# First layer's attention: probabilities scaled while they are turned, by products with a scaled unit matrix

## The chip, the cores and the metric

The kernel runs as one program on one core of a Trainium2 chip. The metric is the device time of one execution in microseconds; shown is the median of several executions. The numbers of the profile come from one execution that the hardware profiler recorded.

## What is computed

The reference is a trunk of two layers over 512 latent tokens and 256 context tokens of width 1024. The first layer runs global attention (eight heads of 64, in two groups that share keys and values) beside a bidirectional RWKV-7 recurrence; the second runs windowed attention beside a state-space mixer. Each layer ends in an MLP. The change is in the first layer's attention, which for a block of queries is:

```python
def block(q):
    s_lat = jnp.einsum('bqgrd,bkgd->bgrqk', q, kl).astype(F32) * scale
    s_ctx = jnp.einsum('bqgrd,bkgd->bgrqk', q, kc).astype(F32) * scale
    p_lat, p_ctx = joint_softmax([s_lat, s_ctx])
    return (jnp.einsum('bgrqk,bkgd->bqgrd', p_lat.astype(vl.dtype), vl)
            + jnp.einsum('bgrqk,bkgd->bqgrd', p_ctx.astype(vc.dtype), vc))
```

The context tokens attend to the context alone, in the same form.

## The kernel before

Everything is F32 on 128 partitions. Tokens are cut into six tiles of 128: tiles 0 and 1 are context, 2 to 5 latent. The order of instructions on each engine is not written out: the code is traced into a list, and a scheduler of the tile framework, which plays a timeline forward, places each instruction on its engine. Code under `tc.high_priority()` (the steps of the recurrence) goes first. Each engine then works through its own list in order.

The stage around the change is the second `with` block (line 886 on). Two things are woven into each other there by generators: the recurrence (`state_mixing`, 12 blocks with two steps each; its products are `z`, `xv`, `x`, `u`, `s` and `y`, lines 985 to 1072) and attention (`attend`, line 1127, one call per tile in the order 0, 1, 3, 4, 2, 5). At its end `finish` normalises the recurrence's output, tile by tile, and turns it (`yt`, line 1116).

`attend` works per tile on two groups of four heads. For each head the scores go into `sc` (line 1147), VectorE finds the row's maximum into `st` (line 1149), ScalarE takes the exponential into `prob` with the row sum beside it (line 1154), VectorE inverts the sum (line 1155), and ScalarE multiplies the whole row of `prob`, 768 columns for a latent tile and 256 for a context tile, by the inverse (line 1156). Then `weighted` (line 323) goes through the tiles of keys, two for a context tile and six for a latent one: four transposes of 128x128, one per head, into one tile `pt` of PSUM (line 332), a copy to SBUF into `pts` by VectorE or ScalarE (lines 335 and 337), and a product with the values into `po` (line 341). These products come in pairs: the first of a pair uses the first 64 columns of the array and writes the upper half of `po`, the second the other columns and the lower half. Lines 344 and 345 add the halves. The second layer's `attend1` calls `weighted` too.

Raw weights are loaded from HBM by SP into three buffers of 128x1024 with the tag `wraw` (line 283) and split into a high and a low part (`split`: ScalarE line 279 into `whi`, VectorE line 280 into `wlo`, two buffers each). After the stage comes the output product `wout` (line 1302), for the context tokens first, then two groups of latent tiles: for each group the mixers' output is loaded back from DRAM (`raw`, line 1293), split into `xr` and other places, and multiplied by eight tiles of weights that go through `wraw`. The queries `qr` and `qs` of `attend` sit in the buffers with the tags `whi` and `wlo`.

Of the kernel before, what the change touches and what calls it, by code (L numbers as in the profile page):

```python
# [10 lines left out]
F32 = mybir.dt.float32  # L11
F32R = mybir.dt.float32r
AF = mybir.ActivationFunctionType
# [5 lines left out]
P = 128  # L19
# [205 lines left out]
def tile_trunk(ctx: ExitStack, tc: tile.TileContext, t: dict, out, cc: Cols, pc: Cols):  # L225
    nc = tc.nc
    V, A, G, T = nc.vector, nc.scalar, nc.gpsimd, nc.tensor

    def pool(name, bufs=1, space=bass.MemoryType.SB, stack=ctx, side="left"):
        waits = "pool" if space == DRAM else "tile"  # L230
        return stack.enter_context(tc.tile_pool(name=name, bufs=bufs, space=space, side=side, reuse_waits=waits))
# [3 lines left out]
    def u(s):  # L235
        uid[0] += 1
        return f"{s}_{uid[0]}"

    cp = pool("const")
    wp = pool("weights")  # L240
# [8 lines left out]
    def K(name, a=0, n=None):  # L249
        s, w = cc.at[name]  # L250
        return cst[:, s + a:s + (w if n is None else a + n)]

    def Q(name, a=0, n=None):
        s, w = pc.at[name]
        return par[:, s + a:s + (w if n is None else a + n)]

    ident, ones = K("ident"), K("ones")
# [8 lines left out]
    def psum(tag, name):  # L266
        if isinstance(banks[tag], str):
            tag = banks[tag]
        v = banks[tag]
        if isinstance(v, list):  # L270

            v.append(v.pop(0))
            v = v[0]
        p, bufs, n, tag = v
        return p.tile([P, 512 * n], F32, tag=tag, name=u(name), bufs=bufs)
# [15 lines left out]
    def cols2(seg):  # L291

        return slice(256 + seg[0], 256 + seg[0] + seg[1])
# [29 lines left out]
    def weighted(prob, vt, g, kts, o, pool):  # L323

        r, po, n = HALVES[g], psum("po", "po"), len(kts)
        pair = []
        for m, kt in enumerate(kts):
            pt = psum("pt", "pt")  # L330
            for j in range(4):
                T.transpose(pt[:, P * j:P * j + P], prob[j][:, P * m:P * m + P], ident)  # L332
            w = pool.tile([P, 512], F32, tag="pts", name=u("pts"), bufs=3)
            if m % 2 == 1:
                V.tensor_copy(out=w, in_=pt)
            else:
                A.activation(out=w, in_=pt, func=AF.Copy)
            pair.append((m, kt, w))
            if len(pair) == 2 or m == n - 1:
                for i, (m_, k_, w_) in enumerate(pair):  # L340
                    T.matmul(po[HALVES[i], :], lhsT=vt[:, k_, r], rhs=w_, start=m_ < 2, stop=m_ + 2 >= n, tile_position=(0, 64 * i))  # L341
                pair = []
            yield
        A.activation(out=o[r], in_=po[HALVES[1], :], func=AF.Copy)
        V.tensor_tensor(out=o[r], in0=po[HALVES[0], :], in1=o[r], op=ALU.add)
# [540 lines left out]
    with ExitStack() as sb:  # L886
# [240 lines left out]
        def attend(qi, keys):  # L1127

            kt0, kt1 = keys
            c0, c1 = 256 + P * kt0, 256 + P * kt1  # L1130

            qr = wp.tile([P, 1024], F32R, tag="whi", name=u("qr"), bufs=2).bitcast(F32).rearrange("p (h c) -> p h c", h=8)
            for o in HALVES:
                nc.sync.dma_start(qr[o], qD[0:4, :, P * qi:P * qi + P].rearrange("j (g q) c -> q (j g) c", g=2))
            qs = wp.tile([P, 1024], F32R, tag="wlo", name=u("qs"), bufs=2).rearrange("p (h c) -> p h c", h=8)
            A.activation(out=qs, in_=qr, func=AF.Copy)
            V.tensor_tensor(out=qs[64:128], in0=qr[64:128], in1=qs[64:128].bitcast(F32), op=ALU.subtract)
            o = tp.tile([P, 512], F32, tag="oa", name=u("oa"), bufs=1)
            for g in (0, 1):
                prob = []  # L1140
                for j in range(4):
                    ps = psum("sc", "sc")
                    for s in SEGS:
                        if s[0] >= P * kt1:
                            continue
                        for m, kx in enumerate((kh, kl)):
                            T.matmul(ps[:, cols2(s)], lhsT=qs[:, 2 * j + g, :], rhs=kx[:, g, s[0]:s[0] + s[1]], start=m == 0, stop=m == 1)  # L1147
                    st = tp.tile([P, 4], F32, tag="st", name=u("st"), bufs=6)
                    V.tensor_reduce(out=st[:, 0:1], in_=ps[:, c0:c1], op=ALU.max, axis=AX.X)
                    sc = sq8[:, qi, 2 * j + g:2 * j + g + 1]  # L1150
                    V.tensor_scalar(out=st[:, 1:2], in0=st[:, 0:1], scalar1=sc, scalar2=-1.0, op0=ALU.mult, op1=ALU.mult)
                    pr = tp.tile([P, NT], F32, tag="prob", name=u("prob"), bufs=5)
                    pv = pr[:, 0:c1 - c0]
                    A.activation(out=pv, in_=ps[:, c0:c1], func=AF.Exp, scale=sc, bias=st[:, 1:2], accum_out=st[:, 2:3])
                    V.reciprocal(out=st[:, 3:4], in_=st[:, 2:3])
                    A.activation(out=pv, in_=pv, func=AF.Copy, scale=st[:, 3:4])
                    prob.append(pr)
                    yield
                yield from weighted(prob, vtok, g, list(range(kt0, kt1)), o, tp)
            nc.scalar.dma_start(oD[0:4, :, P * qi:P * qi + P].rearrange("a q c -> q a c"), o.rearrange("p (a c) -> p a c", c=P))  # L1160
# [105 lines left out]
    with ExitStack() as sc:  # L1266
# [8 lines left out]
        scale = norm_scale(0, 4, "nmlp")  # L1275
# [67 lines left out]
    st = ctx.enter_context(ExitStack())  # L1343
# [6 lines left out]
    def M(name):  # L1350
        return msk[:, mc.at[name][0]:sum(mc.at[name])]

    psum_pool(sd, "right", sc=(1, 2), pt=(1, 1), po=(1, 1))
    with ExitStack() as sh:
# [64 lines left out]
        pk, pv, pb = project((CTX_SEG, *LATS), 8, 9, 0)  # L1419
# [27 lines left out]
        for k in range(KT):  # L1447
            for q, (a, b) in enumerate(((dwh, hh), (dwh, hl), (dwl, hh))):
                for s in SEGS:
                    T.matmul(ps[0:16, cols2(s)], lhsT=a[:, 16 * k:16 * k + 16], rhs=b[:, k, s[0]:s[0] + s[1]],  # L1450
                             start=k == 0 and q == 0, stop=k == KT - 1 and q == 2)
        dr_ = temp("dtraw")
        V.tensor_copy(out=dr_[0:16], in_=ps[0:16, 256:1024])
        pt = psum("s", "dtT")
# [29 lines left out]
        pt = psum("s", "acs")  # L1484
# [17 lines left out]
        def attend1(qi):  # L1502

            lo, hi = max(2, qi - 1), min(NTT, qi + 2)
            n = hi - lo
            kts = [0, 1] + list(range(lo, hi))
            o = tp.tile([P, 640], F32, tag="prob", name=u("oa"), bufs=6)[:, 0:512]
            for g in (0, 1):
                prob = []
                for j in range(4):  # L1510
                    hd = 4 * g + j
                    q = q1[:, g, j, P * (qi - 2):P * (qi - 2) + P]
                    ps = psum("sc", "sc")
                    for m, kx in enumerate((k1h, k1l)):
                        T.matmul(ps[:, 256:512], lhsT=q, rhs=kx[:, g, 0:NCTX], start=m == 0, stop=m == 1)
                        T.matmul(ps[:, 512:512 + P * n], lhsT=q, rhs=kx[:, g, P * lo:P * hi], start=m == 0, stop=m == 1)
                    pr = tp.tile([P, 640], F32, tag="prob", name=u("prob"), bufs=6)
                    pv = pr[:, 0:256 + P * n]
                    A.activation(out=pv, in_=ps[:, 256:512 + P * n], func=AF.Copy, scale=0.125)
                    for kt, m in ((qi - 1, "neg0"), (qi + 1, "neg1")):  # L1520
                        if lo <= kt < hi:
                            blk = pr[:, 256 + P * (kt - lo):256 + P * (kt - lo) + P]
                            G.tensor_tensor(out=blk, in0=blk, in1=M(m), op=ALU.add)
                    st = tp.tile([P, 6], F32, tag="st", name=u("st"), bufs=5)
                    V.tensor_reduce(out=st[:, 0:1], in_=pv, op=ALU.max, axis=AX.X)
                    V.tensor_scalar(out=st[:, 1:2], in0=st[:, 0:1], scalar1=-1.0, scalar2=nsink[:, hd:hd + 1], op0=ALU.mult, op1=ALU.min)
                    A.activation(out=pv, in_=pv, func=AF.Exp, bias=st[:, 1:2], accum_out=st[:, 2:3])
                    A.activation(out=st[:, 3:4], in_=Q("sink", hd, 1), func=AF.Exp, bias=st[:, 1:2])
                    V.tensor_tensor(out=st[:, 4:5], in0=st[:, 2:3], in1=st[:, 3:4], op=ALU.add)
                    V.reciprocal(out=st[:, 5:6], in_=st[:, 4:5])  # L1530
                    A.activation(out=pv, in_=pv, func=AF.Copy, scale=st[:, 5:6])
                    prob.append(pr)
                    yield
                yield from weighted(prob, vt1, g, kts, o, tp)

            split(*(q1[:, m, :, P * (qi - 2):P * (qi - 2) + P] for m in (0, 1)), o.rearrange("p (a c) -> p a c", c=P))
# [209 lines left out]
    with ExitStack() as se:  # L1746
# [6 lines left out]
        scale = norm_scale(1, 4, "nmlp")  # L1753
# [50 lines left out]
```

## Time and profile before

| | before |
|---|---|
| median of 3 runs | 2008.97 us (2008.75 to 2009.16) |
| profiled execution | 2009.51 us |
| its span, first to last instruction | 2007.7 us |
| mean granted clock of TensorE | 0.975 |
| bytes read from HBM / written | 200.00 MB / 25.96 MB |
| queue of the loads by SP and ScalarE (q1), share of 16 engines | 36.1% |

The profile gives for each engine the time in which it had work in hand, and groups of like instructions with their count, mean duration and the idle time ahead of them. A name such as `pt<-cst,prob` says which tile is written and which are read; `cst` is the tile of constants that holds the unit matrix. PE is TensorE and PEld its weight loads, DVE VectorE, ACT ScalarE, POOL GpSimd, SP SyncE, which issues loads and stores. The granted clock is the share of TensorE's full speed that the chip allowed. Records of matmuls overlap, since the next starts before the one ahead has drained, so beside a record's duration the time from one start to the next is of use.

### The profile page before, as it was taken

How to read it: one execution, taken by the hardware profiler on the slowest of the kernel's cores; microseconds unless marked ns; L12 is line 12 of the kernel's file. 1: busy time of each engine (PE TensorE's matmuls, PEld its weight loads, DVE VectorE, ACT ScalarE, POOL GpSimd, SP SyncE). 2: the span in 40 equal slices, each digit the busy share in tenths (PEclk: the TensorE clock that was granted, in tenths of full speed). 3: DMA queues.
4: the chain of work that ended last, by engine and by line, in shares of the span. 5: the costliest groups of instructions: out<-in, count | busy, mean ns of one | idle time of the engine just before them, and what ended most of it. 6: DMA issues, size and time to landing. Idle time of an engine off the chain costs nothing.

```text
span 2007.7 us, 34218 instructions
## 1 busy us (share of the span) xinstructions
PE 1896.6 (94%) x13992; PEld 1545.1 (77%) x13992; DVE 1215.2 (61%) x2150; ACT 840.7 (42%) x1419; POOL 294.2 (15%) x291
## 2 busy tenths in 40 slices
PE   6999988899998999999999999899899789999997
PEld 4776756776765998888888889778578488888886
DVE  5567979775677765654544444865687464444445
ACT  3344442555544552232223224544566454333335
POOL 0000014432321520000000002310153120000001
PEclk9999998899998999999999999999999799999998
DMA  9355575742414733344444422212101133333333
GB/s 336 121 166 171 182 228 148 156 89 56 98 44 132 251 107 99 122 124 136 125 125 121 136 84 80 76 53 74 32 1 53 32 95 105 95 92 97 95 97 113
DMA packets 147884, 228.18 MB, mean 114 GB/s; under 512 B 65024, under 2 KB 102288, under 8 KB 147600
## 3 DMA queue, kind: packets, MB, share of 16 engines
q1 hardware_dynamic: 140912, 213.54, 36.1%
q10 hardware_dynamic: 5456, 7.73, 1.1%
q0 software_dynamic: 1360, 4.73, 0.7%
q8 instruction: 110, 1.80, 0.4%
q14 instruction: 46, 0.38, 0.1%
HBM read 200.00 MB, written 25.96 MB: 113 GB/s over the span
## 4 chain that ended last, share of the span: by engine, by line
PE 77%; DVE 9%; DMA 7%; ACT 3%; issue 3%; POOL 1%; SPq 0%; DVEq 0%; POOLq 0%; ACTq 0%
PE m L367 37%; PE win L367 13%; PE po L341 4%; DMA wmod<-in_wmod_dram 4%; PE pt L332 3%; PE z L985 2%; DVE wlo L280 2%; PE sc L1147 2%; PE wout L1718 1%; PE wout L1302 1%; PE s L1051 1%; PE mod L405 1%; PE lora L653 1%; PE z L1560 1%; DVE junk L1319 1%
## 5 line engine op out<-in xcount | busy, mean ns | idle before, releaser
L279 ACT ACTIVATE whi<-wraw 128x1024 fp32r<-128x1024 f32 x214 | 226.4, 1059 | 678.0 <-PE m L367 561.0
L280 DVE TENSOR_TENSOR wlo<-wraw,whi 128x1024 fp32r<-128x1024 f32 x214 | 264.4, 1236 | 212.2 <-ACT whi L279 209.4
L367 PE MATMUL m<-hh,whi 128*128 128x512 f32 (+1 forms) x816 | 239.3, 344 | 4.9 <-ACT relu L1241 2.4
L367 PE MATMUL m<-hl,whi 128*128 128x512 f32 (+1 forms) x816 | 241.2, 343 | 0.2 <-POOL hl L503 0.2
L367 PE MATMUL m<-hh,wlo 128*128 128x512 f32 (+1 forms) x816 | 241.3, 344 | 0.0
L367 PE MATMUL m<-dl,whi 128*128 128x256 f32 (+1 forms) x832 | 240.7, 341 | 0.0
L367 PE MATMUL m<-dh,whi 128*128 128x256 f32 (+1 forms) x832 | 238.6, 342 | 1.7 <-DVE xl L1223 1.6
L367 PE MATMUL m<-dh,wlo 128*128 128x256 f32 (+1 forms) x832 | 239.8, 341 | 0.1
L367 PEld LDWEIGHTS m<-dh,whi 128*128 128x128 f32 x832 | 153.3, 188 | 23.9 <-DVE xl L1223 4.9
L367 PEld LDWEIGHTS m<-hh,whi 128*128 128x128 f32 x816 | 152.1, 188 | 24.7 <-ACT relu L1241 2.8
L471 POOL TENSOR_TENSOR acc<-acc,nsq 128x256 f32<-128x256 f32 x42 | 42.8, 1027 | 865.8 <-ACT nsq L470 861.0
L367 PEld LDWEIGHTS m<-hl,whi 128*128 128x128 f32 x816 | 153.6, 188 | 19.4 <-POOL hl L503 0.4
L367 PEld LDWEIGHTS m<-dl,whi 128*128 128x128 f32 x832 | 153.8, 188 | 19.0
L367 PEld LDWEIGHTS m<-dh,wlo 128*128 128x128 f32 x832 | 153.7, 188 | 18.9 <-DVE wlo L280 0.3
L367 PEld LDWEIGHTS m<-hh,wlo 128*128 128x128 f32 x816 | 153.4, 188 | 19.0 <-DVE wlo L280 0.3
L367 PE MATMUL win<-hl,whi 128*128 128x512 f32 (+1 forms) x512 | 162.3, 348 | 4.7 <-POOL hl L503 3.5
L367 PE MATMUL win<-hh,whi 128*128 128x512 f32 (+1 forms) x512 | 162.3, 362 | 2.7 <-ACT hh L498 2.7
L367 PE MATMUL win<-hh,wlo 128*128 128x512 f32 (+1 forms) x512 | 160.2, 345 | 0.0
L1319 DVE SCALAR_TENSOR_TENSOR junk<-wmod,crow 128x1024 f32<-128x1024 f32 x64 | 78.5, 1226 | 118.5 <-DMA wmod<-in_wmod_dram 117.9
L1223 DVE SCALAR_TENSOR_TENSOR xl<-m,modT,xl 128x512 f32<-128x512 f32 (+1 forms) x144 | 97.4, 686 | 72.3 <-PE m L367 72.3
L367 PEld LDWEIGHTS win<-hh,whi 128*128 128x128 f32 x512 | 95.4, 194 | 33.6 <-issue 15.7
L367 PEld LDWEIGHTS win<-hl,whi 128*128 128x128 f32 x512 | 98.5, 193 | 22.9 <-issue 5.7
(413 smaller groups left out, 3560.0 us busy)
## 6 DMA issues: line engine op xcount, KB each, us to landing
wraw<-in_w_dram SPq DMA_DIRECT2D x136, 512.0 KB, 3.6
wmod<-in_wmod_dram SPq DMA_DIRECT2D x96, 512.0 KB, 4.2
wraw<-in_wout_dram SPq DMA_DIRECT2D x40, 512.0 KB, 3.7
wraw<-in_win_dram SPq DMA_DIRECT2D x35, 512.0 KB, 4.4
arD<-ar SPq DMA_DIRECT2D x8, 768.0 KB, 4.5
kbD<-kb SPq DMA_DIRECT2D x8, 768.0 KB, 6.5
ari<-arD SPq DMA_DIRECT2D x24, 256.0 KB, 3.9
kbd<-kbD SPq DMA_DIRECT2D x48, 128.0 KB, 3.9
```

The source lines that it names most:

```text
L279: A.activation(out=hi, in_=src, func=AF.Copy)
L280: (lo_eng or V).tensor_tensor(out=lo, in0=src, in1=hi.bitcast(F32), op=ALU.subtract)
L332: T.transpose(pt[:, P * j:P * j + P], prob[j][:, P * m:P * m + P], ident)
L341: T.matmul(po[HALVES[i], :], lhsT=vt[:, k_, r], rhs=w_, start=m_ < 2, stop=m_ + 2 >= n, tile_position=(0, 64 * i))
L367: T.matmul(part(ps, s), lhsT=a[:, c], rhs=row(b, k, s), start=first and j == 0 and q == 0, stop=last and j == n - 1 and q == 2)
L405: T.matmul(ps[r:r + 32, :], lhsT=cs[:, k, :], rhs=wm[:, c], start=k == 0, stop=k == KT - 1, tile_position=(0, r))
L471: (V if k == KT - 1 else eng).tensor_tensor(out=at(acc, s), in0=at(acc, s), in1=at(sq, s), op=ALU.add)
L653: T.matmul(ps[s][d][:, 0:s[1]], lhsT=LORA[wname][r, P * p:P * p + P], rhs=src[r, tokens(s)], start=True, stop=True, tile_position=(64 * d, 0))
L985: T.matmul(ps[:, P * (2 * a + c):P * (2 * a + c) + P], lhsT=kb[:, 2 * m + a, c, :], rhs=ar[:, 2 * m + a, c, :], start=True, stop=True)
L1147: T.matmul(ps[:, cols2(s)], lhsT=qs[:, 2 * j + g, :], rhs=kx[:, g, s[0]:s[0] + s[1]], start=m == 0, stop=m == 1)
L1223: V.scalar_tensor_tensor(out=xs, in0=part(ps, s), scalar=mod(l, which, m, s[2]), in1=xs, op0=ALU.mult, op1=ALU.add)
L1319: V.scalar_tensor_tensor(out=junk, in0=wm, scalar=1.0, in1=crow[:, :, v], op0=ALU.mult, op1=ALU.mult, accum_out=modT[:, l, n, v:v + 1])
```

## The change

The row of `prob` is no longer multiplied by the inverse sum. Instead ScalarE writes, per head, the unit matrix times the inverse sums, a diagonal of 128x128 (`dg`), and `weighted` turns a square of `prob` by a matrix product: the square is the stationary operand, the diagonal the moving one, so that the square comes out turned and each of its columns scaled. The four diagonals of a group share one tile of 128x1024 (512 columns used) from the three `wraw` buffers. The second layer keeps its scaling and its transposes and hands `None` for the diagonal.

```diff
@@ weighted
             for j in range(4):
-                T.transpose(pt[:, P * j:P * j + P], prob[j][:, P * m:P * m + P], ident)
+                pr, dg = prob[j]
+
+                if dg is None:
+                    T.transpose(pt[:, P * j:P * j + P], pr[:, P * m:P * m + P], ident)
+                else:
+                    T.matmul(pt[:, P * j:P * j + P], lhsT=pr[:, P * m:P * m + P], rhs=dg, start=True, stop=True)
@@ attend
                 prob = []
+
+                dgs = wp.tile([P, 1024], F32, tag="wraw", name=u("dg"), bufs=3)
                 for j in range(4):
...
                     V.reciprocal(out=st[:, 3:4], in_=st[:, 2:3])
-                    A.activation(out=pv, in_=pv, func=AF.Copy, scale=st[:, 3:4])
-                    prob.append(pr)
+                    dg = dgs[:, P * j:P * j + P]
+                    A.activation(out=dg, in_=ident, func=AF.Copy, scale=st[:, 3:4])
+                    prob.append((pr, dg))
@@ attend1
-                    prob.append(pr)
+                    prob.append((pr, None))
```

The scheduler places many instructions of the stage anew. Lines behind the edits have numbers that are 5 to 8 higher in the changed kernel. Three places show what moves.

TensorE, within the attention of a latent tile, before: `pt` with its transposes, `sc` the scores of a later group, and the two products of a pair into `po`.

```order
L332 MATMUL pt_4884<-cst,prob_4605 128x128
L332 MATMUL pt_4884<-cst,prob_4670 128x128
L332 MATMUL pt_4884<-cst,prob_4701 128x128
L332 MATMUL pt_4884<-cst,prob_4722 128x128
L1147 MATMUL sc_4987<-kh,qs_4593 128x256
L1147 MATMUL sc_4987<-kl,qs_4593 128x256
L341 MATMUL po_4737<-pts_4843,vtok 64x512
L341 MATMUL po_4737<-pts_4869,vtok 64x512
L332 MATMUL pt_4900<-cst,prob_4605 128x128
```

The same group now (`pt_4909` is its fifth tile of keys, `pts_4878` the second of a pair and `pts_4898` the first of the next):

```order
L346 MATMUL po_4746<-pts_4878,vtok 64x512
L337 MATMUL pt_4909<-dg_4605,prob_4614 128x128
L337 MATMUL pt_4909<-dg_4605,prob_4679 128x128
L337 MATMUL pt_4909<-dg_4605,prob_4710 128x128
L337 MATMUL pt_4909<-dg_4605,prob_4731 128x128
L346 MATMUL po_4746<-pts_4898,vtok 64x512
L337 MATMUL pt_5073<-dg_4931,prob_4940 128x128
```

In the first piece both products of a pair stand side by side; in the second, products into `po` stand alone between those of `pt`. Over the stage 12 of the 28 pairs stood side by side before, and 5 do now.

SP's queue, before, ahead of the stage: loads for the recurrence (`vm`), the second and third load of the output product's weights, and keys (`kraw`).

```order
L965 DMA vm_3272<-vD 32x256
L965 DMA vm_3274<-vD 32x256 x4
L284 DMA wraw_7211<-in_wout_dram 128x1024
L900 DMA kraw_3255<-qD 64x768 x2
L284 DMA wraw_7246<-in_wout_dram 128x1024
L784 DMA ttD<-im_2184 128x1024
```

Now these loads stand behind the last loads of the recurrence, just ahead of the reload of the mixers' output:

```order
L970 DMA vm_3274<-vD 32x256
L284 DMA wraw_7190<-in_wout_dram 128x1024
L284 DMA wraw_7223<-in_wout_dram 128x1024
L284 DMA wraw_7258<-in_wout_dram 128x1024
L284 DMA wraw_7293<-in_wout_dram 128x1024
L284 DMA wraw_7328<-in_wout_dram 128x1024
L1301 DMA raw_7177<-oD 128x4x256
```

Three loads moved from before the stage to its end; the fourth and fifth stood at its end before too, on either side of the first reloads.

TensorE at the stage's end, before: a turned tile of the recurrence (`yt`), the last head's scores, then the last group's transposes between the first output products.

```order
L1116 MATMUL yt_7072<-cst,yacc 128x128 x4
L1147 MATMUL sc_5701<-kh,qs_5245 128x256
L1147 MATMUL sc_5701<-kl,qs_5245 128x256
L1147 MATMUL sc_5701<-kh,qs_5245 128x512
L1147 MATMUL sc_5701<-kl,qs_5245 128x512
L332 MATMUL pt_5725<-cst,prob_5688 128x128
L332 MATMUL pt_5743<-cst,prob_5688 128x128
L1302 MATMUL wout_7184<-xr,whi_7180 128x256 x2
```

Now:

```order
L1075 MATMUL y_7053<-state_6998,ard_3282 64x64
L1077 MATMUL y_7053<-vu_7049,z_3286 64x64
L1077 MATMUL y_7053<-vu_7051,z_3287 64x64
L1121 MATMUL yt_7084<-cst,yacc 128x128 x4
L1310 MATMUL wout_7196<-xr,whi_7192 128x256
L1310 MATMUL wout_7229<-xr,whi_7225 128x256
L1310 MATMUL wout_7196<-xr,whi_7192 128x256
L1310 MATMUL wout_7196<-xr,wlo_7193 128x256
```

All of attention now stands ahead of these rows, and two output products begin together.

## The prediction

> **What bounds the kernel now.** I read the page first, then the busy time of the engines in stretches of the first layer's attention and recurrence (370 to 645 us), then the groups of that stage, then TensorE's timeline.
>
> ```profile
> span 2007.7 us, 34218 instructions
> PE 1896.6 (94%) x13992; PEld 1545.1 (77%) x13992; DVE 1215.2 (61%) x2150; ACT 840.7 (42%) x1419; POOL 294.2 (15%) x291
> 400.00:430.00 30.00, 30.00 (x481) 23.64 (x481) 24.05 (x65) 16.19 (x40) 9.47 (x10) 1.00 0.49 105
> 490.00:520.00 30.00, 30.00 (x431) 22.02 (x431) 18.90 (x42) 16.72 (x32) 8.13 (x8) 1.00 0.38 83
> 520.00:550.00 30.00, 29.80 (x456) 22.69 (x454) 21.30 (x49) 17.87 (x32) 7.46 (x7) 1.00 0.39 95
> 610.00:640.00 30.00, 22.54 (x216) 14.44 (x214) 21.25 (x42) 13.52 (x20) 3.96 (x4) 0.83 0.53 170
> ```
>
> After the 30.00 of each stretch stand TensorE, its weight loads, VectorE, ScalarE and GpSimd; then the granted clock, the DMA share and GB/s. Through the stage TensorE is busy all the time and ScalarE a little over half of it. Only at the stage's end, from 610 us, does TensorE lose 7.5 us. The groups of the stage (busy us, mean ns of one | idle time before them):
>
> ```profile
> L332 PE MATMUL pt<-cst,prob 128*128 128x128 f32 x221 | 41.4, 291 | 0.9 <-ACT prob L1156 0.9
> L1156 ACT ACTIVATE prob<-prob,st 128x768 f32<-128x768 f32 (+1 forms) x48 | 37.9, 789 | 10.6 <-DVE st L1155 10.4
> PEld pt L332: 1.3, 1
> PEld sc L1147: 1.6, 2
> ```
>
> The last two rows are from the view of line 1156, from its list of those who waited for it (us, times). The scaling that the change takes away keeps ScalarE busy for 37.9 us, but TensorE waited for it only some 4 us in all (0.9, 1.3 and 1.6, in part the same moments). So ScalarE is not what this stage is short of; TensorE is.
>
> A busy TensorE can still have room, since records overlap: one of 128 columns lasts about 280 ns. What counts is from one start to the next.
>
> ```profile
> 480.05 1.16 PE L985 MATMUL z<-ari,kbd 128*128 128x128 f32 x8
> 481.05 0.38 PE L332 MATMUL pt<-cst,prob 128*128 128x128 f32 x2
> ...
> 484.35 0.66 PE L332 MATMUL pt<-cst,prob 128*128 128x128 f32 x4
> 484.93 1.07 PE L341 MATMUL po<-pts,vtok 128*64 128x512 f32 x2
> 485.93 0.66 PE L332 MATMUL pt<-cst,prob 128*128 128x128 f32 x4
> ```
>
> Group follows group without a gap, and none of these rows has an idle time behind it. I read this as a queue in which each further record costs its start-to-start time.
>
> **The change part by part.**
>
> (1) *224 transposes become products.* By the loops, six tiles with two groups of heads turn 2x2x2 + 4x2x6 = 56 pt tiles of four squares each; the row above counts 221 of the 224 in its window. What a product costs against a transpose, the kernel shows elsewhere: line 1116 turns 24 squares, line 631 multiplies six squares by the unit matrix as the moving operand, in the same shape and type.
>
> ```profile
> L1116 PE MATMUL yt<-cst,yacc x24: 272/273/329, 501.5 to 647.3; 128*128 128x128 f32 x24
> L631 PE MATMUL kbc<-cst,tbc x12: 270/275/275, 292.5 to 293.8; 128*128 128x128 f32 x12
> 292.54 1.50 PE L631 MATMUL kbc<-cst,tbc 128*128 128x128 f32 x12
> 293.88 0.38 PE L848 MATMUL vtok<-cst,vraw 128*128 128x128 f32 x2
> ```
>
> 24 transposes are 24 records; six products are twelve. A plain f32 product is two passes, a transpose one. In the stage, four products (z, x8) take 481.05 - 480.05 = 1.00 us, four transposes (pt, x4) 484.93 - 484.35 = 0.58 us: 0.42 us more for each of 56 tiles, +23.5 us. From below: six products in 293.88 - 292.54 = 1.34 us are 0.223 us each, against 0.58/4 = 0.145, so 224 x 0.078 = 17.5 us. From above: a whole further record at z's 1.00/8 = 0.125 us, 28 us. I take 23.5, as z stands among the same neighbours. All of it lies on TensorE's queue, and so on the path.
>
> (2) *The order of po.* The order of instructions moves too. The two products that add a pair of turned tiles go to different halves of po; twelve pairs stood next to each other on TensorE before, five do now.
>
> ```profile
> 561.35 1.08 PE L341 MATMUL po<-pts,vtok 128*64 128x512 f32 x4
> 562.36 0.66 PE L332 MATMUL pt<-cst,prob 128*128 128x128 f32 x4
> ```
>
> Two neighbours (x4 records) take 562.36 - 561.35 = 1.01 us; a lone one (x2) took 485.93 - 484.93 = 1.00 us. So neighbours run at once, and each pair that is parted costs 1.0 us: 7 x 1.0 = +7 us. The bound below is 0, if the other half of the array runs something else meanwhile; I take 7, the measured case.
>
> (3) *ScalarE.* 48 scalings go, 48 diagonals of 128 columns come.
>
> ```profile
> L1156 ACT ACTIVATE prob<-prob,st x48: 495/926/940, 371.8 to 634.0; 128x768 f32<-128x768 f32 x32, 128x256 f32<-128x256 f32 x16
> ```
>
> No row shows such a diagonal. 256 columns take 495 ns and 768 take 926, so a straight line gives 0.39 us for 128 (an estimate from these two); above it is the 495, below it nothing. ScalarE is relieved of 37.9 - 48 x 0.39 = 19 us. The path gains at most the 4 us of waits above; most of these change places with the next wait, and I take -1.
>
> (4) *The end of the stage and the weights.* The diagonals live in the three buffers of raw weights. Before, three loads of the output product's weights were issued ahead of the stage, the first and third of them here:
>
> ```profile
> 293.54 0.33 SPq L284 DMA_DIRECT2D wraw<-in_wout_dram  x1
> 337.09 0.54 SPq L284 DMA_DIRECT2D wraw<-in_wout_dram  x1
> wraw<-in_wout_dram SPq DMA_DIRECT2D x14, 512.0 KB, 4.9
> ```
>
> Now five loads stand on SP behind the last loads of the recurrence, the third of them waits for the last diagonal to be read, and behind it is queued the reload of the mixers' output (raw), on which the first output product waits. Such a load lands in 4.9 us. On the other side, attention is now all done before the recurrence ends, where before it hung over:
>
> ```profile
> 626.71 0.44 PE L332 MATMUL pt<-cst,prob 128*128 128x128 f32 x2 [0.86 <-ACT prob L1156]
> 630.63 0.99 ACT L1154 ACTIVATE prob<-sc,st,sq 128x768 f32<-128x768 f32 x1 [3.97 <-DVE st L1151]
> 631.61 1.99 ACT L279 ACTIVATE xr<-raw 128x1024 fp32r<-128x1024 f32 x2
> 632.71 0.58 PE L1302 MATMUL wout<-xr,whi 128*128 128x256 f32 x1 [5.55 <-ACT xr L279]
> 639.08 1.07 PE L341 MATMUL po<-pts,vtok 128*64 128x512 f32 x2
> ...
> L279 ACT ACTIVATE whi<-wraw x21: 1042/1060/1064, 324.2 to 699.8; 128x1024 fp32r<-128x1024 f32 x21
> L280 DVE TENSOR_TENSOR wlo<-wraw,whi x20: 1214/1226/1364, 328.4 to 698.8; 128x1024 fp32r<-128x1024 f32 x20
> ```
>
> The split of raw (xr) stood behind a softmax that had waited 3.97 us for VectorE, and TensorE idled 5.55 us until it. That softmax is out of the way now, but the attention work that filled TensorE from 639 us on is gone too, so the third weight's split (ScalarE 1.06 us, VectorE 1.23 us after the first product frees its buffer) is bare. Bounds: -5.5 us (the idle time goes) to +4.9 us (a load is waited for in full). I take 0, between them, since one split (2.3 us) and part of a load stand against part of the idle time.
>
> (5) *The rest.* One gap inside the stage hangs on the neighbours' order and may go or come:
>
> ```profile
> 440.80 2.07 PE L985 MATMUL z<-ari,kbd 128*128 128x128 f32 x8 [2.32 <-ACT z L994]
> ```
>
> I take 0, with 2.3 us either way. Line 1532 only packs a pair in the second layer and adds no instruction.
>
> Sum: 23.5 + 7 - 1 + 0 + 0 = 29.5 us. The profiled execution took 2009.51 us, 1.8 more than its span, so 2039.0; the median of the runs is 0.54 lower, so I forecast 2038.5 us.
>
> **The rivals.**
>
> *TensorE has room (same).* Its weight loads are busy only 22.02 of 30 us between 490 and 520, so about 8 us in 30 could be free. From 370 to 627 us that would be 68 us, more than the 30.5 to be placed, and the time stays at 2009. The starts speak against it: 484.35, 484.93, 485.93, each when the group before has given out its last record. The Trainium skill, Perfetto Trace Analysis, section "Identifying the Most-Contended Engine", would have TensorE's headroom judged by the weight loads' share and not by matmul occupancy; by that rule this rival holds, and the starts above do not bear it out. 4%.
>
> *ScalarE's chain sets the stage (faster).* If the second pass hides behind the semaphore waits at each change of group, only the reliefs are left: the 4 us of waits on the scaling and the 5.55 us of idle time at the stage's end, 2009 - 9.5 = 1999.5 us. It decides if four products take no longer than the 0.58 us of four transposes; z's 1.00 us and line 631's 1.34 us for six say no. 3%.
>
> *A product costs four transposes.* Then three more records each: 224 x 3 x 0.125 = 84 us, 2093 us. Line 631's twelve records for six products speak against it. The Trainium skill, TensorE: Matmul & The Clock Gate, section "Terms", calls the transpose mode four times faster for FP32, and by that this is the outcome; the records show twice. 2%.
>
> *The weights come late (slower by more).* The end of the stage costs its +4.9 us and the third weight's split 2.3 us on top of a whole second record: 2009 + 28 + 7 + 7.2 = 2051 us. Speaking for it is SP's new order; against it, that loads one and two need only old diagonals. 6%.
>
> **How the numbers follow.** The forecast has the other 85%. The range goes from the lower price of the products with the -1 and the -2.3 us of (3) and (5), without the pairs (17.5 - 3.3: 2023), to the upper price with the pairs and part of the end's cost (28 + 7 + 4: 2048). Those ends leave out the first three rivals, the last one and some of the forecast's own tail. A measurement can tell about 0.2% (4 us) from no change. Slower by more: 0.85 + 0.06 + 0.02 = 0.93; same 0.04; faster 0.03.
>
> **What would show it.** Right: about 224 more TensorE records on the page (some are lost in any trace); eight records of pt in a row taking about 1.0 us; ScalarE's busy time down by some 19 us with no gain; the first layer's attention and recurrence some 30 us longer at full TensorE, and all from the output product on shifted by that. Wrong: pt tiles of four products in 0.6 us; a stage of unchanged length with more records in it; or a TensorE that waits for diagonals, or for weights after the last y.

## The result, and the profile after

The changed kernel takes 2036.06 us (median of four executions) against 2009.07 us for the kernel before on the same chip, 27 us more. Three of the four took 2035.91 to 2036.16 us; the fourth, of 2704.58 us at a granted clock of 0.65, is left out of the ratio, which is 1.0129, 95% interval 1.0114 to 1.0145. The profiled execution took 2036.16 us.

First the page of the changed kernel, the span and the engines' busy time.

```profile
span 2034.4 us, 34684 instructions
PE 1921.3 (94%) x14216; PEld 1573.2 (77%) x14216; DVE 1212.4 (60%) x2150; ACT 825.6 (41%) x1419; POOL 288.9 (14%) x291
```

TensorE has 14216 - 13992 = 224 more records, one for each former transpose, and ScalarE is busy 15 us less on the whole page. The stretches of the stage, in the same columns as before (TensorE, weight loads, VectorE, ScalarE, GpSimd, granted clock):

```profile
400.00:430.00 30.00, 30.00 (x487) 24.68 (x484) 22.19 (x58) 14.64 (x36) 7.65 (x8) 1.00 0.45 100
490.00:520.00 30.00, 29.73 (x387) 22.38 (x389) 17.38 (x41) 14.06 (x32) 6.95 (x7) 1.00 0.31 77
520.00:550.00 30.00, 29.42 (x373) 21.47 (x369) 17.03 (x37) 14.03 (x30) 5.33 (x7) 1.00 0.25 59
640.00:670.00 30.00, 21.30 (x231) 16.08 (x230) 16.89 (x31) 6.87 (x9) 5.41 (x4) 0.89 0.61 184
```

TensorE is as full as it was, and the weight loads are at 22 of 30 us as they were. The end of the stage, where TensorE loses 8.7 us (7.5 before), has moved from 610-640 to 640-670: the stage is some 30 us longer (31.0, counted below). The groups of the stage (busy us, mean ns | idle time before), and ScalarE's line of the diagonals (ns: least, median, most):

```profile
L337 PE MATMUL pt<-dg,prob 128*128 128x128 f32 x444 | 69.8, 290 | 0.0
L346 PE MATMUL po<-pts,vtok 128*64 128x512 f32 x112 | 53.8, 608 | 0.0
```

```profile
L1164 ACT ACTIVATE dg<-cst,st x48: 388/401/407, 366.2 to 635.0; 128x128 f32<-128x128 f32 x48
```

The group of `pt` has grown from 41.4 us (221 records) to 69.8 (444). A diagonal takes 401 ns, where 0.39 us was estimated. What a product costs on the queue is read from one start to the next, here in TensorE's timeline of the changed kernel:

```profile
553.53 1.16 PE L337 MATMUL pt<-dg,prob 128*128 128x128 f32 x8
554.62 0.34 PE L1075 MATMUL y<-state,ard 128*64 128x64 f32 x4
554.79 1.02 PE L346 MATMUL po<-pts,vtok 128*64 128x512 f32 x2
...
563.19 1.16 PE L337 MATMUL pt<-dg,prob 128*128 128x128 f32 x8
564.28 1.07 PE L346 MATMUL po<-pts,vtok 128*64 128x512 f32 x2
```

Four products take 554.62 - 553.53 = 1.09 us, and 1.09 us again at 563.19. Four transposes took 0.58.

The stage's end: SP's loads in the changed kernel, then ScalarE's and TensorE's rows.

```profile
605.41 42.98 SPq L284 DMA_DIRECT2D wraw<-in_wout_dram  x5
653.29 0.38 SPq L1301 DMA_DIRECT2D raw<-oD  x1
656.03 3.75 SPq L1301 DMA_DIRECT2D raw<-oD  x2
```

```profile
622.53 1.06 ACT L279 ACTIVATE whi<-wraw 128x1024 fp32r<-128x1024 f32 x1 [4.83 <-DMA wraw<-in_wout_dram]
661.35 1.06 ACT L279 ACTIVATE xr<-raw 128x1024 fp32r<-128x1024 f32 x1 [1.20 <-DMA raw<-oD]
```

```profile
662.46 0.80 PE L1310 MATMUL wout<-xr,whi 128*128 128x256 f32 x2 [7.57 <-ACT xr L279]
```

The five loads of weights went out between 605.4 and 648.4 us, spread over the last part of the stage, and ScalarE's wait for one of them (4.83 us) fell under a full TensorE. What TensorE then waits for, 7.57 us instead of 5.55, is the reload of the mixers' output: issued at 653.29, and split (`xr`) as soon as it has landed, at 661.35. In the list of transfers (KB each, median us from issue to landing) these reloads became slower, 5.2 us before

```profile
raw<-oD SPq DMA_DIRECT2D x4, 512.0 KB, 5.2
```

and 8.7 us now:

```profile
raw<-oD SPq DMA_DIRECT2D x4, 512.0 KB, 8.7
```

### The profile page after: what moved, and what is told of

Read it like the earlier page. It is cut to its first block, busy times and chain, and to the rows that moved or that the text cites. A ratio compares the mean times of both kernels' runs of the same rounds, so it can differ in the third digit from the quotient of the medians.

```text
span 2034.4 us, 34684 instructions
## 1 busy us (share of the span) xinstructions
PE 1921.3 (94%) x14216; PEld 1573.2 (77%) x14216; DVE 1212.4 (60%) x2150; ACT 825.6 (41%) x1419; POOL 288.9 (14%) x291
## 4 chain that ended last, share of the span: by engine, by line
PE 64%; DVE 8%; DMA 4%; ACT 3%; issue 2%; POOL 1%; SPq 0%; DVEq 0%; POOLq 0%; ACTq 0%
PE m L372 37%; PE win L372 4%; PE po L346 4%; DMA wmod<-in_wmod_dram 3%; PE pt L337 3%; PE wout L1310 2%; PE wout L1726 2%; PE z L990 2%; DVE wlo L280 2%; PE sc L1154 1%; PE s L1056 1%; PE z L1568 1%; DVE junk L1327 1%; PE pt L335 1%; PE y L1077 1%
## 5 line engine op out<-in xcount | busy, mean ns | idle before, releaser
L372 PEld LDWEIGHTS win<-hh,whi 128*128 128x128 f32 x512 | 95.8, 195 | 33.4 <-issue 15.4
```

The source lines that it names most:

```text
L372: T.matmul(part(ps, s), lhsT=a[:, c], rhs=row(b, k, s), start=first and j == 0 and q == 0, stop=last and j == n - 1 and q == 2)
```

## The experiments

**Theory:** the stage is TensorE's queue, and the second record of every product is the whole price. **Rivals:** part of the 27 us comes from the shared buffers, from the diagonals' chain on ScalarE or from the stage's end; ScalarE's relief gives something back; TensorE's order alone makes the difference. All ratios are to the kernel before on the same chip, with their 95% intervals. Since the scheduler lays out the stage anew for each kernel, I also add up TensorE's timeline from 330 us (ahead of the stage) to the first layer's last output product: for each tile the time from each record's start to the next record's start. Where that is over about 0.4 us (0.6 after `po` and `sc`), what exceeds the usual time is put down as a wait. The table below is made so.

| us, start to start | before | after | products alone | products twice | one pass |
|---|---|---|---|---|---|
| `pt` | 33.4 | 62.4 | 61.7 | 113.0 | 35.0 |
| `po` | 42.7 | 46.1 | 43.0 | 46.1 | 44.8 |
| waits inside the stage | 15.9 | 12.4 | 20.0 | 13.0 | 14.9 |
| waits ahead of and between `wout` | 9.2 | 14.4 | 13.5 | 19.9 | 11.0 |
| all, 330 us to last `wout` | 388.1 | 413.7 | 424.6 | 472.3 | 383.5 |

**Products alone.** The kernel before, with products by the plain unit matrix in the first layer; ScalarE's scaling stays and no diagonals are made.

```diff
-    def weighted(prob, vt, g, kts, o, pool):
+    def weighted(prob, vt, g, kts, o, pool, plain=None):
...
-                T.transpose(pt[:, P * j:P * j + P], prob[j][:, P * m:P * m + P], ident)
+                if vt is plain:
+                    T.matmul(pt[:, P * j:P * j + P], lhsT=prob[j][:, P * m:P * m + P], rhs=ident, start=True, stop=True)
+                else:
+                    T.transpose(pt[:, P * j:P * j + P], prob[j][:, P * m:P * m + P], ident)
...
-                yield from weighted(prob, vtok, g, list(range(kt0, kt1)), o, tp)
+                yield from weighted(prob, vtok, g, list(range(kt0, kt1)), o, tp, vtok)
```

> The kernel before with only its 224 transposes turned into products with the plain unit matrix; ScalarE still scales, no diagonals, the raw weights keep their three buffers and their early loads. Theory (the second pass alone makes the cost): 2009 + 23 to 29, with up to 5 us for pairs of po (7 of 28 neighbours): 2032 to 2043 us. Rival (late weights make a part of the cost): below 2030 us. Rival (ScalarE's relief gives something back in the changed kernel): 2040 us or more.

Measured: 2049.62 us, 1.0204 (1.0181 to 1.0227), outside the window of the theory by some 7 us and in that of the second rival. The products themselves cost what they should, `pt` +28.3 us. But the kernel with less of the change in it is 13.6 us slower than the whole change, 6.7 of it in waits. Either ScalarE's relief is worth that much once the products are there, or the arrangement is. Later runs take this up.

**Products twice.** The changed kernel with each product issued twice in a row into the same place.

```diff
                     T.matmul(pt[:, P * j:P * j + P], lhsT=pr[:, P * m:P * m + P], rhs=dg, start=True, stop=True)
+                    T.matmul(pt[:, P * j:P * j + P], lhsT=pr[:, P * m:P * m + P], rhs=dg, start=True, stop=True)
```

> The changed kernel with each of the 224 products issued twice into the same place. Theory (each record costs its start-to-start time on a full queue): 448 more records at 0.112 to 0.125 us, 50 to 56 us over the changed kernel's 2036: 2086 to 2092 us. Rival (TensorE has room, the first step was paid in waits or order): less than half of that, 2060 us or less.

Measured: 2094.18 us, 1.0426 (1.0407 to 1.0446). The 448 further records take 113.0 - 62.4 = 50.6 us of the queue, 0.113 us each, and the time rises by 58 us, 2 us beyond the theory's window; most of the rest is at the stage's end, where the waits grow from 14.4 to 19.9 us. Its timeline, where line 338 is the second issue:

```profile
547.44 0.39 PE L337 MATMUL pt<-dg,prob 128*128 128x128 f32 x2
547.66 0.39 PE L338 MATMUL pt<-dg,prob 128*128 128x128 f32 x2
547.89 0.39 PE L337 MATMUL pt<-dg,prob 128*128 128x128 f32 x2
548.11 0.39 PE L338 MATMUL pt<-dg,prob 128*128 128x128 f32 x2
```

A product follows a product after 0.22 us. There is no room in TensorE that a further record could use for nothing.

**One pass.** The changed kernel with `prob` and the diagonals in F32R; the probabilities and the inverse sums are rounded to that type, and the products are otherwise the same.

```diff
-                dgs = wp.tile([P, 1024], F32, tag="wraw", name=u("dg"), bufs=3)
+                dgs = wp.tile([P, 1024], F32R, tag="wraw", name=u("dg"), bufs=3)
...
-                    pr = tp.tile([P, NT], F32, tag="prob", name=u("prob"), bufs=5)
+                    pr = tp.tile([P, NT], F32R, tag="prob", name=u("prob"), bufs=5)
```

> The changed kernel with the probabilities and the diagonals rounded to F32R (lower precision), so that the product is one pass. Theory: 224 records of 128 columns in place of 448, as many as the transposes were and none dearer: the second pass's 23 to 29 us go, the loads of weights stay late: 2003 to 2013 us. Rival (buffers and order make the cost): 2025 us or more.

Measured: 2007.64 us, 0.9989 (0.9978 to 1.0000). Diagonals, shared buffers, ScalarE's relief and products are all there, and the 27 us are gone. Line 337 of this kernel, and four of its products in the timeline:

```profile
L337 PE MATMUL pt<-dg,prob x224: 219/276/331, 369.9 to 639.7; 128*128 128x128 f32 x112
```

```profile
549.06 0.66 PE L337 MATMUL pt<-dg,prob 128*128 128x128 f32 x4
549.65 1.07 PE L346 MATMUL po<-pts,vtok 128*64 128x512 f32 x2
550.65 0.66 PE L337 MATMUL pt<-dg,prob 128*128 128x128 f32 x4
551.15 0.33 PE L1154 MATMUL sc<-kh,qs 128*128 128x256 f32 x1
```

One record per product, and 0.50 to 0.59 us for four, as for transposes. So it is the second record that costs, not the product as such. As fast as the kernel before at a lower precision is no gain.

**Half the dose.** The changed kernel with products for the first group of heads (g = 0); the second group keeps scaling and transposes.

```diff
-                dgs = wp.tile([P, 1024], F32, tag="wraw", name=u("dg"), bufs=3)
+                if g == 0:
+                    dgs = wp.tile([P, 1024], F32, tag="wraw", name=u("dg"), bufs=3)
...
-                    dg = dgs[:, P * j:P * j + P]
-                    A.activation(out=dg, in_=ident, func=AF.Copy, scale=st[:, 3:4])
+                    if g == 0:
+                        dg = dgs[:, P * j:P * j + P]
+                        A.activation(out=dg, in_=ident, func=AF.Copy, scale=st[:, 3:4])
+                    else:
+                        dg = None
+                        A.activation(out=pv, in_=pv, func=AF.Copy, scale=st[:, 3:4])
```

> The changed kernel with the products in the first half of the heads only (g = 0); the other half is scaled by ScalarE and transposed as before. So 112 of the 224 additional TensorE records are left. Theory (TensorE sets the stage, every additional record costs its own 0.11 to 0.13 us): 112 x 0.13 = 14.6 us over the kernel before, so 2019 to 2029 us. Rival (the cost is a fixed one of the new buffers, of the diagonals' chain or of the stage's end, which half the products pay in full): 2032 us or more. Rival that the products are hidden while few of them come: 2014 us or less.

Measured: 2028.89 us, 1.0085 (1.0067 to 1.0102), at the upper edge of the theory's window. Start to start, `pt` is 47.4 us, half-way between 33.4 and 62.4. The queue follows the dose; the time (17 us for half) does so only roughly.

**Relief alone.** The kernel before without its scaling; the division by the sums is left out of the first layer's attention.

```diff
-                    A.activation(out=pv, in_=pv, func=AF.Copy, scale=st[:, 3:4])
```

> The kernel before without the scaling by the inverse sum in the first layer (the division is left out); the transposes stay. It shows what relieving ScalarE of 37.9 us of busy time is worth by itself. Theory (TensorE's queue is full, ScalarE hides): 2009 us, give or take 5; the neighbouring pairs of po fall from 12 to 8 of 28, which costs up to 4 us. Rival (ScalarE's chain sets the stage): 1999 us or less.

Measured: 2016.18 us, 1.0036 (1.0022 to 1.0050). Nothing is gained by 48 fewer instructions on ScalarE; it is even 7 us slower, and 2 us beyond the theory's window. Where TensorE waits in this kernel (us in total, times, longest):

```profile
PE wout L1301 <- ACT xr L279: 9.7, 1, 9.7
PE y L1072 <- DVE vu L1041: 4.5, 4, 1.8
PE z L985 <- ACT z L994: 4.0, 2, 3.3
```

No wait for `prob` is among them, and the one at the stage's end has grown from 5.6 to 9.7 us, with the products nowhere in this kernel.

**Products unscaled.** Products with the plain unit matrix and no scaling (the division is left out), to be held against the products alone, to which the diff is.

```diff
-                    A.activation(out=pv, in_=pv, func=AF.Copy, scale=st[:, 3:4])
```

> The products with the plain unit matrix (as in the run with the products alone), and the scaling on ScalarE left out as well; no diagonals are made, so the division by the sums is left out of the first layer's attention. Theory A (ScalarE's relief gives time once the products have lengthened TensorE's work; that is why the changed kernel is 13 us faster than the products alone): 2040 us or less, near the changed kernel's 2036. Theory B (relief gives nothing here either; the 13 us are the order in which the stage's end fell out): within 5 us of the products alone, 2044 to 2055.

Measured: 2042.10 us, 1.0161 (1.0146 to 1.0176), between the two windows: by the medians 7.5 us of the 13.6 come back when ScalarE is relieved (9 of 15 by the ratios).

**Scaling kept too.** The changed kernel with a pass of the old size put back on ScalarE.

```diff
+                    A.activation(out=pv, in_=pv, func=AF.Copy, scale=1.0)
                     dg = dgs[:, P * j:P * j + P]
```

> The changed kernel with ScalarE's pass over the probabilities put back beside the diagonal (a scaling by 1.0, the same 48 instructions of the same size), so ScalarE gets some 34 us more work and the results are the same. Theory A (the relief is worth about 13 us in the changed kernel): 2045 us or more. Theory B (ScalarE waits anyway, its work is under TensorE's): 2036 us, 5 us either way.

Measured: 2044.11 us, 1.0170 (1.0155 to 1.0185): 8 us slower than the changed kernel, just under the bound of theory A. With the run before, two pairs for a relief worth some 8 us; against them stands the relief alone.

**Diagonals idle.** The kernel before, with the diagonals made in the shared buffers and not used.

```diff
+                dgs = wp.tile([P, 1024], F32, tag="wraw", name=u("dg"), bufs=3)
...
                     A.activation(out=pv, in_=pv, func=AF.Copy, scale=st[:, 3:4])
+                    A.activation(out=dgs[:, P * j:P * j + P], in_=ident, func=AF.Copy, scale=st[:, 3:4])
```

> The kernel before with the diagonals made in the buffers of the loaded weights, but not used: transposes and scaling stay. It has the diagonals' 48 ScalarE instructions and the shared buffers without the products. Theory (both lie beside TensorE's work): 2009 us, 6 us either way. Rival (the shared buffers hold up the next layer's weights, or the diagonals ScalarE's chain): 2016 us or more.

Measured: 2005.15 us, 0.9976 (0.9967 to 0.9986). With 48 more instructions on ScalarE and the buffers shared, the kernel is 5 us faster. The buffers cost nothing here. Nothing in the edit can save time by itself. In its trace 3.7 us are gained ahead of the stage (the recurrence's first product stands at 346.5 us instead of 350.2) and 2.1 us in it, and 1.9 us are lost behind it. I take this for the arrangement and for what differs from one execution to another; no run separates the two.

**Unit copies, transposed.** The whole change, but transposes in the products' place, with plain copies of the unit matrix as diagonals (the division is left out).

```diff
-                    T.matmul(pt[:, P * j:P * j + P], lhsT=pr[:, P * m:P * m + P], rhs=dg, start=True, stop=True)
+                    T.transpose(pt[:, P * j:P * j + P], pr[:, P * m:P * m + P], dg)
...
-                    A.activation(out=dg, in_=ident, func=AF.Copy, scale=st[:, 3:4])
+                    A.activation(out=dg, in_=ident, func=AF.Copy, scale=1.0)
```

> The changed kernel with transposes in the products' place and plain copies of the unit matrix in the diagonals' buffers, so the division by the sums is left out of the first layer's attention. It has everything of the change (ScalarE's relief, the diagonals' instructions, the shared buffers) but the products. Theory (only the products cost): 2009 us, 6 us either way. Rival (the shared buffers or the diagonals' chain hold part of the 27 us): 2020 us or more. Rival (the relief is a gain that the products hide): 1999 us or less.

Measured: 2022.59 us, 1.0063 (1.0041 to 1.0085), 14 us above the kernel before and by the number in the first rival's window. The groups and the waits of this kernel say where they are:

```profile
L346 PE MATMUL po<-pts,vtok 128*64 128x512 f32 x112 | 56.4, 608 | 0.1
L337 PE MATMUL pt<-dg,prob 128*128 128x128 f32 x224 | 41.1, 285 | 0.9 <-ACT prob L1161 0.8
```

```profile
PE wout L1310 <- ACT xr L279: 6.2, 1, 6.2
PE wout L1310 <- DVE wlo L280: 4.6, 6, 2.3
```

The transposes cost what they did (31.8 us start to start); `po` costs 50.3 instead of 42.7, as 3 of its 28 pairs stand side by side instead of 12; the wait for weights' low parts is 4.6 us instead of 2.0. None of it is a wait for diagonals. The 2.6 us more for the weights may belong to the shared buffers; this run doesn't separate that.

**Arrangement alone.** To see what another arrangement is worth, one column per head is copied on VectorE, 48 times 150 ns, into a place that is used up: once in the kernel before, once in the changed kernel.

```diff
+                    V.tensor_copy(out=st[:, 0:1], in_=st[:, 2:3])
                     V.reciprocal(out=st[:, 3:4], in_=st[:, 2:3])
```

> The kernel before with one copy of a single column per head put on VectorE (48 in all, the sum over a maximum that is used up; the results are the same). It is there to make the scheduler arrange the stage otherwise, with almost no work of its own. If the arrangement is worth nothing: 2009 us, 2 us either way. If differences of 5 to 8 us between kernels are within what the arrangement alone gives: up to 8 us away from 2009 on either side.

Measured: 2020.17 us, 1.0053 (1.0033 to 1.0072): 11 us, more than either window.

> The changed kernel with the same single-column copies on VectorE, so that the scheduler arranges the stage otherwise. If the arrangement is worth nothing: 2036 us, 2 us either way; if it is worth several us: 2028 to 2046.

Measured: 2051.52 us, 1.0202 (1.0175 to 1.0229): 15 us above the changed kernel, again beyond the window. The stretch from 330 us to the last output product, first of the kernel before, then of it with the copies:

```profile
330.00:718.10 388.10, 367.70 (x4612) 288.25 (x4611) 288.64 (x613) 201.54 (x374) 129.69 (x111) 0.96 0.47 124
```

```profile
330.00:729.20 399.20, 369.79 (x4612) 287.44 (x4611) 289.56 (x664) 202.00 (x374) 128.70 (x111) 0.97 0.46 121
```

The same 4612 records of TensorE take 2 us more, and the idle time grows from 20.4 to 29.4 us. Of the changed kernel, and of that with the copies:

```profile
330.00:743.70 413.70, 390.39 (x4808) 312.78 (x4807) 279.21 (x595) 185.48 (x374) 125.50 (x110) 0.98 0.45 118
```

```profile
330.00:755.40 425.40, 397.40 (x4793) 316.32 (x4792) 282.66 (x638) 183.72 (x371) 125.33 (x111) 0.97 0.43 113
```

Here TensorE is busy 7.0 us longer and idle 28.0 instead of 23.3 us.

**A second pair for the relief.** The last kernel with ScalarE's pass put back as in the run "scaling kept too".

> The run before this one (changed kernel, single-column copies) with ScalarE's pass over the probabilities put back as a scaling by 1.0: a second pair for the worth of the relief, in another arrangement. Theory A (the relief is worth about 8 us once the products are there): 5 to 11 us slower than that run. Theory B (the 8 us of the first pair were the arrangement): a difference under 4 us, or of the other sign.

Measured: 2041.78 us, 1.0149 (1.0113 to 1.0184): 10 us faster with more work on ScalarE, the other sign. So theory A isn't borne out. The copies are in both kernels of this pair, so they can't be what cost the changed kernel its 15 us either, at least not by themselves; that each head's chain is 0.15 us longer remains a possible part of the 11 us in the kernel before, and wasn't taken apart.

**The runs together.** The relief was tried in four pairs; its worth came out, by the ratios, as -7, +9, +8 and -11 us. By ratio, the six kernels with one record per turned square (the kernel before among them) lie at 0.9976 to 1.0063, the six with two records at 1.0129 to 1.0204. The groups don't touch. Their means, 1.0020 and 1.0169, are 0.0149 apart, which is 30 us; within each group, kernels that differ by a few small instructions scatter over 15 to 17 us. The half dose lies between them, at 1.0085. The traces say the same of the stage alone, from the recurrence's first product to the last output product: 366 to 380 us with one record, 399 to 413 with two, 390 with the half dose and 457 with products twice.

## Why the prediction was right

The forecast was 2038.5 us, the result 2036.06, within the range and by the mechanism named. The terms did not each come out as forecast, and that the sum is no more than 2.4 us off is partly luck: misses in (1), (2), (4) and (5) offset each other.

(1) *Products for transposes: under-sized.* Forecast 23.5 us, between 17.5 and 28; measured 62.4 - 33.4 = 29.0 us, and 28.3 with the products alone. What failed is the choice of z's 1.00 us for four products, less the transposes' 0.58. In place it is 1.09 us, 0.51 above four transposes and 28.6 us over 56 tiles, so the upper row (a whole further record) was the right one. The two records per product were right, so the rival of four transposes falls. The Trainium skill, TensorE: Matmul & The Clock Gate, section "Terms", calls the transpose mode four times faster for FP32; here it is one record against two, and 0.58 us against 1.09 from start to start. The Trainium skill, Perfetto Trace Analysis, section "Transposes", asks that a logical transpose be issued as one and not as a matmul; the runs agree, at 0.13 us a square in F32, while in F32R the matmul costs hardly more (35.0 us against 33.4 for all 224).

(2) *The order of po: right in kind, over-sized.* By the busy time of its group `po` grew from 46.8 to 53.8 us, the 7 us of the forecast; by starts only 42.7 to 46.1, 3.4 us. A parted product often has other records slipped in beside it, so a parted pair doesn't cost the full 1.0 us. Over all fourteen kernels `po` goes from 41.8 us (13 pairs side by side) to 50.3 (3 pairs), a straight line through them falling by about 0.75 us a pair, with exceptions (43.0 us at 7 pairs).

(3) *ScalarE: right.* Its busy time on the page fell by 15 us instead of 19; by the two groups alone, 37.9 us of scalings against 48 diagonals of 401 ns, it is the 19. Less work there gained nothing that stands out of the arrangement's scatter. Whether the 1 us taken for waits on `prob` was gained can't be told within that scatter. The rival in which ScalarE's chain sets the stage falls with the relief alone and with the one-pass run, neither of which came near 1999.5 us.

(4) *The stage's end: dearer than 0, for another reason.* The waits ahead of and between the output products rose from 9.2 to 14.4 us, +5.2, just past the upper bound of +4.9. The mechanism was wrong: the third of the five loads of weights was to wait for the last diagonal. But the loads went out one by one as diagonals were read, the third at 621.7 us, and only the fifth after the last product of `pt` (647.7 us). So the rival of the late weights falls. TensorE's largest waits there are now these (us in total, times, longest):

```profile
PE wout L1310 <- ACT xr L279: 7.6, 1, 7.6
PE wout L1310 <- DVE wlo L280: 3.3, 4, 1.6
PE wout L1310 <- DVE oy L1125: 1.7, 1, 1.7
```

Before, they were 5.6, 2.0 and none. So 2.0 us more go to the split of the reload, 1.3 to the weights' low parts, and 1.7 are put down to VectorE's work on the turned tiles. The softmax that had stood ahead of the split is gone, as forecast, but the reload itself took its place: it lands late, 8.7 us after its issue instead of 5.2. Why it is slower wasn't tried; the relief alone, which has no products, has a wait of 9.7 us there as well.

(5) *The gap in the stage: within its bounds, and more around it.* Waits inside the stage fell from 15.9 to 12.4 us. The records of all other tiles but `wout` (+1.4) are 9.9 us shorter. Together: 29.0 + 3.4 + 5.2 - 3.5 + 1.4 - 9.9 = 25.6 us in the stretch, and 1.0 behind it, against 26.7 us of the spans.

But the stretch begins at 330 us in both kernels, and the changed kernel is further on by then. It reaches the recurrence's first product (`z`) at 344.8 us, the kernel before at 350.2, each with 2493 records of TensorE behind it. So 5.4 us of what the waits and the other records lost lie ahead of the stage. From that product to the last output product, before and after:

```profile
350.20:718.10 367.90, 348.11 (x4501) 272.07 (x4501) 269.13 (x559) 197.18 (x365) 124.35 (x109) 0.96 0.46 120
344.80:743.70 398.90, 376.20 (x4725) 300.97 (x4725) 265.11 (x559) 181.12 (x365) 120.93 (x108) 0.98 0.44 115
```

The stage has 224 more records and is 31.0 us longer, 1.5 above the 29.5 forecast. The total came out below the forecast since 5.4 us were saved ahead of the stage, for which the prediction has no term. The change puts no work there. Up to that point the granted clock is 0.98 instead of 0.97, and three loads have moved away; what saved the time wasn't tried. In the other twelve kernels the same product stands at 342.7 to 350.3 us. Of the rest of the shorter records `z` has 3.3 us; in the stage too the granted clock is higher, 0.98 instead of 0.96, and what share it has stays open.

*TensorE has room* falls most clearly: 448 further records cost 58 us with the weight loads at 77 to 78% of the span all the while. For this stage the rule of the weight loads' share (the Trainium skill, Perfetto Trace Analysis, section "Identifying the Most-Contended Engine") showed room that wasn't there, and the start-to-start times didn't.

What the prediction lacked is the arrangement as a term of its own. An estimate of plus or minus 8 us for it, as the two groups scatter, would have been as large as all its terms but the first.

## What to carry to other kernels

Where a stage is one engine's queue, price an edit by that engine's starts, and take the neighbouring records of the same kind at full cost: moving work there from an engine that waits anyway was here a loss of the whole amount. Before folding a scaling into a transpose, look at how many records the product takes in its type. And where a scheduler lays out the stage, give each kernel a control that only rearranges it; differences of half a per cent said nothing about the edit here, and what two pairs agreed on, two others contradicted.

## What the runs showed of the hardware

- An F32R product of 128x128 by 128x128 takes one record and 0.50 to 0.59 us for four, an F32 product two records and 1.09 us for four, an F32 transpose one record and 0.58 us for four, from start to start.
- Each of the two weight loads of a product's 128x128 F32 square takes 192 ns (median of 224 in the half-dose run), that of a transpose 141 ns in the same kernel, the second layer's included. Two rows of that run show it; no run shows whether the difference matters for the time.

```profile
L337 PEld LDWEIGHTS pt<-dg,prob x224: 186/192/193, 370.1 to 620.9; 128*128 128x128 f32 x112
...
L335 PEld LDWEIGHTS pt<-cst,prob x256: 137/141/231, 385.8 to 1625.9; 128*128 128x128 f32 x128
```

- The reloads of 512 KB at the stage's end land in 7.0 to 10.2 us (medians in the twelve kernels of the experiments, with products and without), where the changed kernel has 8.7 and the kernel before 5.2: its own was the exception.
